# Attention on one core: another written-out order of the instructions, with other places for the early transfers, and two start-up copies of k that swap engines

## The chip, the cores and the metric

The kernel runs on one core of a Trainium2 chip. The metric is the device time of one launch in microseconds; lower is better. The engines of the core that matter here are TensorE (PE; its weight loads are listed as PEld), VectorE (DVE), ScalarE (ACT), GpSimd (POOL) and SyncE (SP), which only issues transfers. Each engine works through its own queue in order and waits for the others by semaphores.

## The reference

Grouped-query attention with 8 batches, 8 query heads, 2 key/value heads, 1024 positions and a head dimension of 64, in float32. Four query heads share one head of k and v.

```python
scale = 1.0 / np.sqrt(head_dim)
for g in range(n_kv_heads):
    q_group = q[:, q_start:q_end, :, :].copy()
    ...
    scores = scale * np.matmul(q_group, k_group.transpose(0, 1, 3, 2))
    scores_max = np.max(scores, axis=-1, keepdims=True)
    attn = np.exp(scores - scores_max)
    attn = attn / (np.sum(attn, axis=-1, keepdims=True) + 1e-08)
    output[:, q_start:q_end, :, :] = np.matmul(attn, v_group)
```

## The kernel before

A *job* is one query head of one batch; there are 64. The scores of a job are computed turned (keys in the partitions, queries along the free axis) in 8 chunks of 128 keys. A chunk is one *tile* of 128 x 1024 scores in one of three PSUM slots (`sp0` to `sp2`), written by two matmuls (L400). So there are 512 tiles, and each has to be raised to e. Two engines share that:

- 366 tiles go to ACT, one exponential each (L411, letter `x` in the order below), into one of 34 buffers `pt`.
- 146 tiles go to DVE, which builds e^x out of bits. The step `p` (L422) writes a scaled score as a 16-bit integer into the ring `ye` of 22 tiles. One or two neighbouring tiles form a *chain*. For a chain, `z` (L431) takes the fraction bits into the ring `zz`; a multiply of `zz` by `ye` follows, part of its columns on POOL (`G`, L448) and the rest on DVE (`m`, L457); `t` (L463) masks `ye` in place, which leaves the exponent part. The two rings together stand for e^x, and PE takes both as terms of one sum; for the last three jobs `+` (L474) adds them first.

PE then multiplies the tiles of a job with v (L491, letter `V`, three small products of 65 columns at a time; column 65 is a row of ones, which gives the sum of the weights). 7 output pieces of 128 queries share a PSUM bank; when they are done DVE takes the reciprocal of the sums (`r`, L560) and scales the pieces (`n`, L571), and SP stores a finished job (`S`). The first job is summed chunk by chunk as its tiles come (`E`, L529), the last one likewise (`L`). `F` is a small matmul on a zero tile, which keeps PE busy early on.

Transfers: POOL's queue issues casts of q, k and v to bf16 in DRAM (`X`/`q`, `Y`/`k`, `Z`/`v`; the capital ones first wait for the latest score matmul). SP's queue issues the turning loads of q (`T`) and k (`K`), the copy of k to the other half of the partitions (`C`) and the fill of v (`U`). A cast `qd8`, from job 6 on, brings two jobs at once; `kd` and `vd` are k and v of a batch and group.

What sets the order is a text, `ORDER`: one letter per step, walked once from left to right. `A` is the score of the next tile for ACT, `a` to `g` the score of a tile for DVE of the current job or up to six jobs ahead; the number is the PSUM slot. `G2,78` means that POOL multiplies 8 x 78 columns of the chain before the one before the last. `LENGTHS` gives the number of tiles in each chain. Every step goes into its engine's queue at the place where the walk meets it. A `G` besides waits for the DVE step that came before the latest `z`, `m`, `t` or `+`:

```python
tc.add_manual_dep(gps.ins, gate.ins.name, Sync, reason="the port goes to the step behind it")
```

Before the walk comes a written-out start (L280 to L313): k and q of job 0 are loaded straight, turned by PE against an identity, and copied out of PSUM into `k0` and `q0` by ACT and DVE.

Of the kernel before, what the change touches and what calls it, by code (L numbers as in the profile page):

```python
# [25 lines left out]
VVVVVG0,108nxd2A0TpVSVVxVVVVA1zd2xA0TG1,148pVVVVVxVVVVA1rnd2xA0pVSVVVVxVG0,36VVVA1zk2e2xA0pVVVG1,47V
VxVVVVVA1zq16d2xA0t3VVVVVG2,115rVxVpVA1VVVVxVVVnA0d2m2xVSVG1,71VpA1TVVxVVVVA0t2e2xG1,78pA1VVVVVxUVVA
0rze2TxVVG2,107VKpA1VVxVVVVVnA0A2xzq18VSVVVVVt3Ve1xA0G2,84pTVVVVCVxVVVA2rzd1xA0G3,172pVVVVVxVVVVVA2n
e1xA0pVVVVVVxVVVA2v2rt3A1xVVVm2VVVVVVVxe0A2G1,192pVVVxVVVVTA1ne0xA2pVSVVVVxVVVVA1rt2e0q20xA2pVVVG1,4
7VVxVVVVA1m1G0,106e0nxA2pVSVVVVxUVVVA1ze0xA2G1,78pVVVVVxVVVA1rze0xA2G2,72pVVVVxVVVTA1t3e0xVG1,192VpA  # L30
2VVVxVVA1ne0xVVpVSA2VVCVxVVVrA1m1q22A0t2xVVVVVt1VTVVVxVVG0,32nd2A1zVSVxVVG1,71A0pVVVxVVKVVA1zd2xA0G2
,78rpVVVVVxVVVVA1zd2xA0G3,75pTVVVVVxVVVA1nG2,18A2xVzVk3VSVVVVVt4Vxd0A1G3,191rpTVVVVxVVVVA2ne0xA1pVSV
VVVVxVVVA2m2q24A0xVVVVVVVrVt2xVVVVA1G3,30nd2xA0m3G1,71pSTVVVVVxVVVA1t3d2xA0G1,79pVVVVVxVVA1rzA2xVVVm
2VVVVVG1,106nd0xUA1pVVVVVxVVCVVA2m1q26A0xVVKVt2VVTVVVVxVt1d1A2G0,72pVVxVVVA0VVzxVv3VVVA1Tzd2xA0G2,18
4rpVVVVVxVVVVA1nd2xA0pSVVVVVxVVVVrA1t2d2xA0G1,71pVVVVVxVVVVzA1q28A2xVzVVVVVG3,114nd0xA1pVSVVVxVVVVA2
rTm3A0xG2,30VnVVVVVt3Se1xA2G2,71pVVVVVxVVVA0m2e1xA2G1,78pTVVVVVxVUVVA0rt2d1xA2G1,178pVVVVxVVVVA0nTd1
xA2pSVVVVVxVVVA0q30zA1CxVzVVVVVVVrG2,106nxd2A0pVVSVVxVVVVA1t3d2xA0KG2,71pVVVVVxVVVA1ze2xA0G3,79pVVVV
VxVVVA1rTzA2k4xVVt4VVVVVVG3,115xne0A1pVSVVxVVA2VVrVxm3Vq32VVVA0m2A1xVVVVVVVTVVG1,106nxe2A0pVSVVVxVVV
VVA1Tt3d2xA0G1,78pVVVVVVxVVVA1rt2A2xVVVm1VVVVG0,107nd0xA1pVVVVVxVVVVA2t1d0xVG0,78VpTA1VVVxVUVVA2rzA0
xVVq34zVVVVVVnxe1G2,71A2pVSVVVxVVKVVA0CG1,10rne1G1,98xA2pVVSVVVxVVVVA0t2v4e1xA2pTVVG1,47VVVxVVVA0ze1  # L40
xA2G2,78pVVVVVxVVVA0rm2G1,106e1nxA2pTVSVVVxVVVVA0t2e1xA2G1,71pVVVVVxVVVA0m1q36A1zxVVVVVG1,122VrVnVxd
2A0pSVVVVxVVVVA1t2e2xA0G1,71pVVVVVxVVVVA1ze2xA0G2,63pVVVVVVxVUVVVTzA1e2xG2,78rA0pVVVVVVxVVVA1t3A2xVz
VVVVTVVVG3,114ne0xA1pVSVVVxVVVKVA2rm3A0q38xzVVVVVVt4e1CxA2G3,225pVVVVVxVVVTA0nd1xA2rpSVVVVVxVVVVA0ne
1xA2m3G2,71SpVVVVVxVVVVA0t3k5A1xVVm2VVVVe2xG1,78A0rpVVVVVxVVVVA1zq40A2xVVzVVVVVVG3,106ne0xA1pVTVVVVx
VVVVA2t4e0xA1G3,72pVVVVVxVVVVVA2rG2,105ne0xA1pSVVVVVVxVUVVVm2A2e0xA1G1,78pVVVVVVxVVVA2rTt3d0xVVVG1,7
# [50 lines left out]
def kernel(  # L96
# [213 lines left out]
    nc.vector.tensor_copy(out=q0[:, 0, h:HS], in_=s0[:, 1, h:HS])  # L310
    nc.vector.tensor_copy(out=k0[:, 0, 0:128], in_=s2[:, 0, 0:128])
    nc.scalar.activation(out=k0[:, 0, 128:HS], in_=ops[1][:, 128:HS], func=AF.Copy)
    nc.vector.tensor_copy(out=k0[:, 1, :], in_=ops[0])  # L313
# [293 lines left out]
```

## Time and profile before

| | |
|---|---|
| runs | 352.6, 352.64, 353.29 us; median 352.64 |
| profiled execution | 352.72 us; its span, first to last instruction, 350.9 us |
| granted clock of TensorE, mean | 0.995 |
| first exponential on ACT starts | 6.27 us after the span's start |
| POOL's issues of casts | 52 in the queue; 128 GB/s mean over all transfers |

The span is what the profile covers; 1.8 us of the profiled time lie around it. In the profile's lines a row of the timeline has the start in the span, the duration, the engine, the line of the kernel, the operation, the tiles written and read, and a count of equal neighbours. A row of the groups has the busy time of all its instructions, the mean length of one in ns, and the idle time of the engine just before them. Instructions of one engine overlap by some 0.08 us, so a mean length is a little more than the step costs in a full queue.

### The profile page before, as it was taken

What the parts mean: (1) busy time and instruction counts of PE and PEld (TensorE: products, weight loads), DVE (VectorE), ACT (ScalarE), POOL (GpSimd) and SP (SyncE); (2) the same over time, 40 slices, a digit from 0 to 9 for tenths busy, and PEclk for the clock granted to TensorE, in tenths of its full rate; (3) what the DMA queues carried; (4) which work ended last, traced back from release to release, by engine and by line L of the source; (5) the groups of instructions that cost most, each with busy time, mean ns of one, the idle gap of its engine ahead of it and who ended that gap; (6) DMA issues with size and microseconds to landing.
All of it is one profiled execution on the core that took longest, in us unless ns stands there. A gap on an engine that the chain in (4) does not pass through costs nothing.

```text
span 350.9 us, 14187 instructions
## 1 busy us (share of the span) xinstructions
PE 340.2 (97%) x6268; PEld 225.7 (64%) x6268; DVE 342.1 (97%) x518; ACT 339.8 (97%) x370; POOL 288.6 (82%) x236
## 2 busy tenths in 40 slices
...
GB/s 150 123 151 178 108 152 138 137 135 95 149 147 116 154 151 131 118 131 138 147 122 112 151 156 133 119 136 158 122 136 138 116 148 98 113 83 86 48 84 102
DMA packets 96606, 44.84 MB, mean 128 GB/s; under 512 B 61184, under 2 KB 95360, under 8 KB 95744
## 3 DMA queue, kind: packets, MB, share of 16 engines
...
q8 instruction: 49, 0.80, 1.0%
...
q14 instruction: 13, 0.11, 0.2%
...
## 4 chain that ended last, share of the span: by engine, by line
PE 55%; DVE 30%; ACT 8%; issue 3%; DMA 2%; SPq 0%; DVEq 0%
PE ops L491 30%; PE sp L400 24%; DVE ye L422 15%; ACT pt L411 8%; DVE ye L463 4%; DVE zz L431 4%; DVE ost L571 3%; DVE zz L457 3%; DMA kt<-kd 2%; DVE rec L560 1%; PE ops L269 1%; PE sp L529 1%; PE sp L292 0%; DVE kt L313 0%; PE ops L304 0%
## 5 line engine op out<-in xcount | busy, mean ns | idle before, releaser
L411 ACT ACTIVATE pt<-sp 128x1024 bf16<-128x1024 f32 x366 | 337.3, 1052 | 3.4 <-PE sp L400 3.2
L448 POOL TENSOR_TENSOR zz<-ye,zz 128x568 bf16<-128x568 bf16 (+29 forms) x126 | 248.5, 1973 | 25.4 <-DVE zz L431 9.0
L422 DVE TENSOR_SCALAR ye<-sp 128x1024 uint16<-128x1024 f32 x146 | 177.1, 1213 | 1.3 <-PE sp L400 0.8
L400 PE MATMUL sp<-qt,kt 64*128 64x512 bf16 x1024 | 166.5, 383 | 4.3 <-ACT pt L411 3.0
L491 PE MATMUL ops<-va,pt 128*128 128x65 bf16 x2832 | 160.6, 194 | 0.0
L491 PEld LDWEIGHTS <-pt 128*128 128x128 bf16 x2832 | 120.5, 98 | 30.7 <-issue 30.7
L491 PE MATMUL ops<-va,zz 128*128 128x65 bf16 x1136 | 123.8, 194 | 0.0
L491 PE MATMUL ops<-va,ye 128*128 128x65 bf16 x1104 | 119.6, 194 | 1.3 <-DVE ye L463 1.3
L491 PEld LDWEIGHTS <-ye 128*128 128x128 bf16 x1104 | 83.9, 98 | 16.9 <-issue 14.8
L491 PEld LDWEIGHTS <-zz 128*128 128x128 bf16 x1136 | 86.5, 98 | 9.8 <-issue 9.5
L400 PEld LDWEIGHTS <-kt 64*128 64x128 bf16 x1024 | 51.6, 93 | 58.9 <-issue 34.9
L463 DVE TENSOR_SCALAR ye<-ye 128x2048 uint16<-128x2048 uint16 (+1 forms) x77 | 51.6, 676 | 0.0
L431 DVE TENSOR_SCALAR zz<-ye 128x2048 uint16<-128x2048 uint16 (+1 forms) x77 | 49.7, 657 | 0.1
L571 DVE TENSOR_TENSOR ost<-ops,rec 128x448 f32<-128x448 f32 (+2 forms) x73 | 44.4, 608 | 0.3
L457 DVE TENSOR_TENSOR zz<-ye,zz 128x2048 bf16<-128x2048 bf16 (+31 forms) x54 | 33.4, 622 | 0.0
L174 POOL DMA_DIRECT2D qd<-in_q_dram x34 | 23.7, 697 | 5.6 <-PE sp L400 4.6
L560 DVE RECIPROCAL rec<-ops 128x7 f32<-128x7 f32 (+2 forms) x73 | 14.1, 194 | 0.0
L443 POOL MEMSET tick<- 128x1 bf16 x52 | 9.7, 187 | 0.0
L174 POOL DMA_DIRECT2D vd<-in_v_dram x8 | 5.9, 735 | 0.0
L174 POOL DMA_DIRECT2D kd<-in_k_dram x8 | 5.7, 712 | 0.0
L269 PE MATMUL ops<-warm 128*128 128x512 bf16 (+1 forms) x12 | 3.5, 448 | 1.2 <-DVE warm L168 1.2
L529 PEld LDWEIGHTS <-pt 128*128 128x128 bf16 x96 | 3.4, 98 | 1.2 <-issue 1.2
...
## 6 DMA issues: line engine op xcount, KB each, us to landing
...
qt<-qd SPq DMA_TRANSPOSE x63, 4.2
...
```

The costliest lines, as they stand in the source:

```text
L174: return nc.gpsimd.dma_start(out=t.rearrange("(a x) d -> a (x d)", a=128), in_=src.rearrange("(a x) d -> a (x d)", a=128),)
L400: now = nc.tensor.matmul(sps[x][:, hf, :], lhsT=t[lo : lo + D, c // NH, ci % NH * 128 : (ci % NH + 1) * 128], rhs=qt[j][lo : lo + D, 0, :] ...
L411: exps.append(nc.scalar.activation(out=p, in_=where_s[(j, c)], func=AF.Exp, scale=scale))
L422: vec = nc.vector.tensor_scalar(out=ye[:, i, :, :], in0=where_s[(j, c)], scalar1=EXP_A, scalar2=EXP_B, op0=ALU.mult, op1=ALU.add,)
L431: vec = nc.vector.tensor_scalar(out=ch.tiles(zz), in0=ch.tiles(ye), scalar1=0x7F, scalar2=0x3F00, op0=ALU.bitwise_and, op1=ALU.bitwise_or,)
L443: tock = nc.gpsimd.memset(tick, 0.0) if any(old) else None
L448: gps = nc.gpsimd.tensor_tensor(out=z, in0=flat(ch.tiles(ye))[:, ch.cols : ch.cols + w], in1=z, op=ALU.mult)
L457: vec = nc.vector.tensor_tensor(out=z, in0=flat(ch.tiles(ye))[:, 0 : ch.cols], in1=z, op=ALU.mult)
L463: vec = nc.vector.tensor_scalar(out=ch.tiles(ye), in0=ch.tiles(ye), scalar1=0x7F80, scalar2=None, op0=ALU.bitwise_and,)
L491: ended[job] = nc.tensor.matmul(ops[g % 2][:, lo : lo + D + 1], lhsT=p[:, par, qs * 128 : (qs + 1) * 128], rhs=va[(b * G + h // HPG) % NVA ...
L560: vec = nc.vector.reciprocal(out=to, in_=sums)
L571: vec = nc.vector.tensor_tensor(out=to, in0=src, in1=by, op=ALU.mult)
```

## The change

`ORDER` and `LENGTHS` are replaced as a whole; the work is the same. There are still 366 exponentials and 146 tiles of DVE. There are 76 chains for 77 (70 of two tiles and 6 of one, for 69 and 8), 120 multiplies on POOL for 126 with 100256 columns for 99344, 58 multiplies on DVE for 54, and 6 of the small matmuls `F` for 3. The beginning of the text, before and after:

```diff
 ORDER = """
-A0IX3TY1a1xA2pxA0za1xKA2pX4E0E2TxFA0m0E3xA1za2t1E5FxpFA0E1xm0A1E6X5zxb2t1A0pE7E4xTA1rzxb2nG0,78A0pxX
-6A1Y2m1xb2A0G0,50pxA1Tt1Z1xA2zb0VVVt1VxVVG0,78VpA1VVxVVVVrA2zc0TG1,101xnVVCpA1SVVxVVVVX8VKA2rm1A0xG0
-,31nVVb1t1v1UxA2pVG0,46VVVVxVVVVA0m0Tq10c1zxA2VpVG0,56VVVVxVVVVA0t1Tc1xzA2G1,200pVVVVVVxVVVVA0rnc1xA
+A0IX3TY1a1xA2pxA0za1xA2TpX4E0E2xFA0m0E3xb1KzA2pE5FxFFA0E6m0xFA1b2zE7X5xpFA0xA1t2Tb2zE1pxG0,56A0xt2b1
+X6A2m1E4xG0,72pA0xA2rnb1Y2t1xA0zVTVVVpVxVG0,170VA2VVVxVVrCnb0A1pTVVxSVA2VVVVm0xVX8VVVt1A0b1t0Z1xA2rV
+zVVVv1VVxVVpVA0TVG0,145VxVVVA2nb1VxUVpA0VVVVxVVKA2m0q10A1VzxVVVVVVVt1Vc0xG0,191A2rpVVVVVxVVVTA1nc0xA
...
@@
-    nc.vector.tensor_copy(out=k0[:, 0, 0:128], in_=s2[:, 0, 0:128])
-    nc.scalar.activation(out=k0[:, 0, 128:HS], in_=ops[1][:, 128:HS], func=AF.Copy)
+    nc.scalar.activation(out=k0[:, 0, 0:128], in_=s2[:, 0, 0:128], func=AF.Copy)
+    nc.vector.tensor_copy(out=k0[:, 0, 128:HS], in_=ops[1][:, 128:HS])
     nc.vector.tensor_copy(out=k0[:, 1, :], in_=ops[0])
```

The first place is the start. DVE's queue before, from the copy of the second half of q0 to the first `p`:

```order
L310 CAST qt<-sp_141 128x256
L311 CAST kt<-sp_143 128x128
L313 CAST kt<-ops_126 128x512
L422 TENSOR_SCALAR ye<-sp_177 128x1024
L431 TENSOR_SCALAR zz<-ye 128x1024
```

DVE's queue there after the change:

```order
L310 CAST qt<-sp_141 128x256
L312 CAST kt<-ops_127 128x384
L313 CAST kt<-ops_126 128x512
L422 TENSOR_SCALAR ye<-sp_177 128x1024
L431 TENSOR_SCALAR zz<-ye 128x1024
```

The copy of 384 columns stands where that of 128 stood; ACT has the one of 128 where it had the one of 384.

The second place is POOL's queue from the first multiply of chain 4 on, some 19 to 25 us into the span before (`L174` rows are casts that it issues). Before:

```order
L448 TENSOR_TENSOR zz<-ye,zz 128x624
L448 TENSOR_TENSOR zz<-ye,zz 128x808
L174 DMA qd_491<-in_q_dram 16x8192
L448 TENSOR_TENSOR zz<-ye,zz 128x248
L174 DMA vd_0_522<-in_v_dram 16x8192
L448 TENSOR_TENSOR zz<-ye,zz 128x368
L174 DMA qd_566<-in_q_dram 16x8192
```

After, from the multiply of chain 4 to that of chain 5:

```order
L448 TENSOR_TENSOR zz<-ye,zz 128x1360
L174 DMA qd_487<-in_q_dram 16x8192
L174 DMA vd_1_507<-in_v_dram 16x4096
L174 DMA vd_0_529<-in_v_dram 16x8192
L448 TENSOR_TENSOR zz<-ye,zz 128x1160
```

Chain 4 has one multiply for two, three casts follow on it in a row (the cast of v for group 1 stood earlier before), and chain 5 has one multiply of 1160 columns where it had two, of 248 and 368, with a cast between them.

The third place is DVE's queue around chain 4's `t` (the `L463` of 2048 columns). Before, from the `p` of tile 7:

```order
L422 TENSOR_SCALAR ye<-sp_449 128x1024
L560 RECIPROCAL rec<-ops_393 128x7
L457 TENSOR_TENSOR zz<-ye,zz 128x616
L571 TENSOR_TENSOR ost<-ops_393,rec 128x448
L463 TENSOR_SCALAR ye<-ye 128x2048
L422 TENSOR_SCALAR ye<-sp_518 128x1024
```

After, from the same tile's `p`:

```order
L422 TENSOR_SCALAR ye<-sp_445 128x1024
L457 TENSOR_TENSOR zz<-ye,zz 128x688
L463 TENSOR_SCALAR ye<-ye 128x1024
L463 TENSOR_SCALAR ye<-ye 128x2048
L560 RECIPROCAL rec<-ops_392 128x7
L431 TENSOR_SCALAR zz<-ye 128x2048
L422 TENSOR_SCALAR ye<-sp_503 128x1024
```

Chain 3's `t` now stands directly ahead of chain 4's, and chain 5, which has two tiles for one, is begun (`L431`) behind it and not ahead of it.

More of the change, by code (lines that the diff above doesn't have):

```diff
@@ L26 @@
[L26 to L45, printed above, removed]
@@ new lines @@
+2pSVVVVxVVVVm0q12A1c0zxA2pVG0,64VVVxVVVVA1rt1c0xVA2G0,192pVVVxVVVTA1nc0xA2pSVVVVVxVVVA1rzc0xA2pVG0,5
+6VVVCVxVVA1t1d0xVG0,184pA2TVVVxA1nc0xpA2STVVVVVxVUVVVVm0q14zA1c0xrA2pG0,63VVVVVVxVVVA1t1c0xVG0,106Vp
+A2VVVxVA1nA0xzVk2VSVVVVVVzVc2xA1G2,78rKpVVVVVxVVVVVA0m2G1,105nc2xA1pVSVVVVVxVVVVA0t2Tq16d2xA1zVVVVG2
+,78pVVxVVVVTA0VVxVrVm2VA1G1,106nc2xVVpA0SVVVxVVVA1m1A2TxVVVt2VVVVVVVt1xc0A1G0,78pVVVVxVVVVVA2rzc0xA1
+TG1,178VpVVVVCVxVVVVA2nc0xA1pVSVVVVVxVVVVA2q18rt1d0xA1KpG0,93VVVVVxVVUVVA2nA0xVzv2VVVVVVzxe1A2G2,80T
@@ new lines @@
+pVVVVxVVVA0rm2d1xA2G1,73pVVVVVxVVVA0t2e1xA2G1,183pVVVVVxVVVA0Tnd1xVVpVSA2VVxVVA0rq20t1A1VxVVzVVVVVVG
+1,106nxd2A0pVSVVVxVVVVVA1ze2xA0G2,71pTVVVVVxVVVVA1m2A2rxt2VVVVVVG1,111Vnd0xUA1pSVVVVVxVVVVTA2ze0xA1G
+2,78pVVVVVxVVVVA2rzq22e0xA1pVVG3,47VVCVxVVKVVA2m3G2,114nd0xA1pSVVVVVxVVVA2rt3e0xVVG2,106pA1TVVVxVVVV
+A2ne0xVm2VG1,71SVpA1VVxVVVA2t2k3e0xA1pVG1,54VVVVxVVVrA2m1e0xA1G0,106pTVVVVxVVVA2nA0xVzVq24VSVVVVt2d1
+xA2G1,71pVVVVxVVVVVA0ze1xA2G2,71pVVVVVVxVVVVA0m2re1t2xA2G1,191pVTVVVVVxUVVVA0nd1xA2pSVVVVVxVVVVA0rze
@@ new lines @@
+1xA2G2,65pTVVVVCVxVVVA0q26zA1xVt3VVVVVG2,114nd2xA0pVVVVxVVVKVA1rzA2v3xA0zVVVVVVxVm4VVVVVVVG3,106ne1x
+A2pVTSVVVVVxVVVVA0t4d1xA2G3,71pVVVVVVxVVVA0m3e1G2,247rxVpVVTA2VxVVA0nd1VxpVVSA2VVVxVVrVnA0A1xVm2Sq28
+t3VVVVVVt2xd2A0TG1,71pVVxVVVVA1zd2xA0G2,78pVVVVVxVVVVVA1rm2d2xA0G1,71pVVVVVVxVUVVA1t2e2xVG1,106VpVA0
+VVxVVVVTnA1A2CxzVq30VSVVVVVzVd0xA1G3,79pVVVVVxVVKVVVA2rne0G2,100xA1pVSVVVVVxVVVA2t3e0xG2,78A1pTVVVVV
+xVVVA2rm2k4A0xzVVVVVVt3Vxd1A2G2,197pVVVVxVVVVA0ne1xA2pSVVTVVVxVVA0rm1A1q32xVVVVVTVVVG2,30nVxVVVm2A2S
@@ new lines @@
+t1d0xVVG0,78VpA1VVxVVVA2rt2e0xA1G0,71pVVVVVxVVVVA2Tzd0xA1G1,107pVVVVVxVUVVVA2nA0xzVVVVVVVVt2Vxe1KA2G
+1,191rpVVVVxVVVVA0ne1CxA2pSVVVVxVVVVTA0m1q34A1zxVVVVVv4t2VVxe2A0rpG1,177VVVVxVVVA1ne2xA0pSVVVVVxVVVA
+1ze2xA0G2,79pVVVVxVVVA1rzA2xVVG2,30VnVVVVVt3q36xSe0A1pVVG2,47VxVVVVVA2Tze0xA1G3,78pVVVVVVxVVVVA2rm3A
+0xVG2,30VnVVTVVVVt3e1xSUA2G2,71pVVVVVxVVVVA0zd1xA2G3,71pVVVVVxVVVA0zd1xA2G4,71pVVVVVxVVVA0m4q38rA1t4
+xVVVKTzVVCVVxe2G4,114nA0VpVVSVxVVVA1VrxVm4VVVA2TG3,106ne0xA1pVSVVVVxVVVA2t4e0xA1G3,79pVVVVVxVVVA2rm3
@@ new lines @@
+k5A0xzVVVVVVt4Vd1xA2G3,227pTVVVVVxVVVVA0ne1xA2rpSVVVVVxVVVA0nA1xVm1q40VVVVVVxe2A0m3G2,78pVVVVxVVVVA1
+rt3e2xA0G2,178VpVVVVxVVUVVA1nd2xA0pVSVVVVVxVVVVA1t1e2xA0G0,71pTVVVVVVxVVVVt2A1e2xG0,84A0rpTVVVVVxVVV
+VA1zq42A2xVVm1VVVCVVG0,115nd0xA1pVSVVVVxVVKVVA2rzA0v5xVVVzVVVVVVxVt3VVVA1G2,106nd2xA0pTSVVVVVxVVVVzA
+1d2xm3A0G2,71pTVVVVVxVVVVA1t3e2xA0G2,121pVVVVVxVVVA1rnA2xVVVVzVSq44VVVVxe0m3A1G2,190rpVVVVVxVVVTVA2n
+d0xA1pSVVVVVVxVVVVA2t3e0xA1G2,66pVVVVVVxVVVzA2e0xG2,114rA1pVVVVVxVUVVTA2nA0xVt3VVSVVVVVq46m2VxVVVVVz
@@ new lines @@
+A1d2xG2,191rA0pVVVVVVxVVA1nCe2VxVpVSVA0VVxVVVm2A1e2t3xVVVVG1,78KpA0VVxVVVVA1rt2e2xA0G1,178pVVVVVxVVV
+VA1nTe2xA0pVVVVVxVVVA1k6zTA2xVVzVVq48VVVVt3Vxe0A1G2,191rpVVVxVVVVVA2nd0xA1pVSVVVVxVVVVA2Tzd0xA1G3,65
+pVVVVVxVVVA2rt3A0xVVVzVVVVVG3,106e1nxA2pVVVSVVxVVVVA0ze1xA2G4,78pVVVVVVxVVUVVA0rm4A1q50xVzVKVVVVVVt5
+xe2A0G4,191pVVVVCVxVVVA1ne2xA0pSVTTVVVVxVVVVA1rm4v6A2xzVVVVVVVt5e0xA1G4,191pVVVVVxVVVVA2nd0xA1rpSVVV
+VVVxVVVm4A2A0G3,30nxA1t4q52VVSVVVxVm2VVVVVVVxc2A0G3,192rpVTVVVVxVVVVA1ne2xA0pSVVVVVVxVVVA1m3e2t2xVVV
@@ new lines @@
+VG1,71pA0VVxVUVVVA1t3e2xA0G1,78pTVVVVxVVVVVrA1zd2xA0G2,107pVVVVVVxVVVA1TnA2xVzVq54VSVVVVt3e0xA1KG2,7
+8pVCVVVVxVVVVA2rzd0xA1G3,178pVVVVVxVVVVTA2nd0xA1pVVVVVxVVVVrA2t3d0xA1G2,106pVVVVVxVVVTA2nA0xVm1Vk7SV
+VVVe1xA2G2,78pVVVVxVVVVA0rm2q56A1xt1VVVVVVt2e2xA0G0,71pVVVxVVVVA1ze2xA0G1,185pVVVVVxVVVVA1nTe2xrA0pS
+VVVVVxVUVVA1ze2xVG1,106VpA0VVVxVVA1nA2Vxm1VVSVVVVVVq58t2Ve0xA1pVVG0,59VVVxVVVVVA2rt1d0xA1G0,106pVVVV
+VVxVVVVA2TnCA0xVzVv7VSVVVVze1xA2KG2,78pVVVVVxVVVVA0rm2e1G1,106nxA2VpVVSVVVxVVVVTA0t2d1xA2G1,78pVVVVV
@@ new lines @@
+VxVVVVTA0rm1A1q60xVzVVVVVVG1,109Vnd2xA0pSVVVVVxVVVVA1t2e2xA0G1,78pVVVVVxVVVVA1Trm1A2xVzVVVVVG1,109Vn
+d0xA1pSVVVVVxVVVVA2t2e0xA1G1,78pVVVVVxVVVA2rze0xVVG2,69VpA1VVxUVVVA2nG1,24A0xzVq62VVVTVVt3Vxe1A2G2,1
+91rpVVVxVVVVA0nCe1xKA2pVSVVVVxVVVA0m2q63A1zxVVVVt3VVe2xG2,118A0rpTVVVVVxVVVA1nA2xVm1VVSVVVVd0xA1G2,7
+1pVVVVVxVVVVA2t1e0xA1G2,67pVVVVVxVVVVVA2rt2d0xA1G0,106pVVVVVVxVVVA2nA0xVzVVSVTVVVVzVxVVVVzA1e2xG3,11
+4VrVpA0VVVxVVVA1ne2xm3A0G2,71SpVVVVVxUVVVVA1t3Td2xG2,81A0pVVVVVxVVA1rzA2xVVVm3VVVVG2,106nd0CxA1pVSVV
```

32 lines of the change are left out of this document (6 added, 26 removed).

## The prediction

> **What bounds the kernel now.** I read the page's busy shares first, then the busy time by stretches, then the timeline of each engine in the one stretch that stands out. The page's first section, and then the stretches (us from the span's start; length, busy time and instructions of PE, PEld, DVE, ACT, POOL; granted clock; DMA share; GB/s):
>
> ```profile
> span 350.9 us, 14187 instructions
> PE 340.2 (97%) x6268; PEld 225.7 (64%) x6268; DVE 342.1 (97%) x518; ACT 339.8 (97%) x370; POOL 288.6 (82%) x236
> ```
>
> ```profile
> 20.00:25.00 5.00, 4.08 (x65) 2.33 (x61) 5.00 (x9) 5.00 (x7) 4.88 (x6) 1.00 0.87 152
> 25.00:30.00 5.00, 4.29 (x61) 2.91 (x63) 4.54 (x7) 2.57 (x3) 2.49 (x4) 0.66 1.11 183
> 30.00:35.00 5.00, 4.89 (x95) 3.12 (x92) 4.58 (x6) 4.87 (x6) 4.06 (x2) 1.00 1.01 157
> 60.00:340.00 280.00, 278.91 (x5300) 188.18 (x5300) 279.45 (x414) 279.82 (x305) 244.54 (x194) 1.00 0.67 125
> ```
>
> From 60 to 340 us three engines are full at once: DVE lacks 0.55 us of 280, ACT 0.18, PE 1.09. Nothing can be won there except by taking work away. Between 25 and 35 us it is different: ACT lacks 2.43 + 0.13 us and PE runs at 0.66 of its clock. The timelines of ACT, DVE and POOL there (start, duration, what; in brackets the idle time before it and what ended it), and the line of the waits between 12 and 35 us for PE:
>
> ```profile
> 27.22 1.94 ACT L411 ACTIVATE pt<-sp 128x1024 bf16<-128x1024 f32 x2 [1.59 <-PE sp L400]
> 30.13 11.16 ACT L411 ACTIVATE pt<-sp 128x1024 bf16<-128x1024 f32 x12 [0.97 <-PE sp L400]
> ```
>
> ```profile
> 23.33 2.33 DVE L463 TENSOR_SCALAR ye<-ye 128x2048 uint16<-128x2048 uint16 x1
> ...
> 30.35 1.22 DVE L422 TENSOR_SCALAR ye<-sp 128x1024 uint16<-128x1024 f32 x1 [0.81 <-PE sp L400]
> ```
>
> ```profile
> 20.66 1.86 POOL L448 TENSOR_TENSOR zz<-ye,zz 128x808 bf16<-128x808 bf16 x1
> 22.46 0.55 POOL L174 DMA_DIRECT2D qd<-in_q_dram  x1
> 23.03 0.66 POOL L448 TENSOR_TENSOR zz<-ye,zz 128x248 bf16<-128x248 bf16 x1
> 23.64 0.55 POOL L174 DMA_DIRECT2D vd<-in_v_dram  x1
> 24.20 0.89 POOL L448 TENSOR_TENSOR zz<-ye,zz 128x368 bf16<-128x368 bf16 x1
> 25.03 0.72 POOL L174 DMA_DIRECT2D qd<-in_q_dram  x1
> ```
>
> ```profile
> PE ops L491 <- DVE ye L463: 1.3, 1, 1.3
> ```
>
> A `t` step of 2048 columns (L463, the masking of ye) lasts 2.33 us. It begins inside POOL's multiply of 248 columns and ends 0.57 us after the multiply of 368 columns has ended (24.20 + 0.89 = 25.09; 23.33 + 2.33 = 25.66), as if it had run only from there. Its own wait, on chain 4's multiplies, was over at 22.52, when the one of 808 columns ended (20.66 + 1.86). So DVE was held by a train of POOL instructions (multiply, cast issue, multiply). PE then waits 1.3 us for this `t`, its clock drops, ACT waits 1.59 and 0.97 us for scores, and DVE itself waits 0.81 us.
>
> **The change, part by part.** Durations, by shape (busy us of the group, mean ns of one, idle before):
>
> ```profile
> L463 DVE TENSOR_SCALAR ye<-ye 128x2048 uint16<-128x2048 uint16 x69 | 48.2, 704 | 0.0
> L431 DVE TENSOR_SCALAR zz<-ye 128x2048 uint16<-128x2048 uint16 x69 | 46.3, 684 | 0.0
> L457 DVE TENSOR_TENSOR zz<-ye,zz 128x2048 bf16<-128x2048 bf16 x9 | 10.8, 1214 | 0.0
> L448 POOL TENSOR_TENSOR zz<-ye,zz 128x624 bf16<-128x624 bf16 x17 | 29.2, 1719 | 3.3 <-DVE zz L431 1.6 <-DVE ye L422 0.8
> L448 POOL TENSOR_TENSOR zz<-ye,zz 128x848 bf16<-128x848 bf16 x10 | 20.6, 2058 | 1.7 <-DVE zz L431 1.4
> L463 DVE TENSOR_SCALAR ye<-ye 128x1024 uint16<-128x1024 uint16 x8 | 3.4, 438 | 0.0
> L457 DVE TENSOR_TENSOR zz<-ye,zz 128x1024 bf16<-128x1024 bf16 x5 | 3.4, 683 | 0.0
> L431 DVE TENSOR_SCALAR zz<-ye 128x1024 uint16<-128x1024 uint16 x8 | 3.4, 421 | 0.0
> ```
>
> *The place of the long `t`.* In the new order chain 4 gets one multiply of 1360 columns on POOL. Chain 5 is begun only after chain 4's `t`, so none of its multiplies can stand ahead of that `t`. POOL's queue there holds the issues of qd8, vd1 and vd0 behind the 1360, and the next multiply (1160 columns) waits for a step of DVE that itself comes after the `t`. The train multiply, cast, multiply is gone from this place. Such a `t` lasts 0.70 us by the mean, so 2.33 - 0.70 = 1.63 us return, and with them DVE's 0.81 us of waiting: 2.44 us. ACT's side gives 1.59 + 0.97 = 2.56, which agrees. PE's idle time of the three stretches is 0.92 + 0.71 + 0.11 = 1.74 us, and its lower clock from 25 to 30 us holds up to 5 x 0.34 = 1.7 more, so PE can follow. Since all three engines are full later, time won here should reach the end.
>
> By the Trainium skill (SBUF — State Buffer, "Who interferes with whom"), GpSimd and a VectorE step in a two-port mode share one pair of ports; the one that issues first holds it for its whole instruction, and the other is blocked. By that, the `t` would have begun when the multiply of 248 ended; the trace shows it held over two more POOL instructions, so it agrees on the block and not on its length. By the rule a block in the new burst would cost one issue at most, 0.55 us, and the sum below would then be 350.1 + 0.55 = 350.6 and not the 352.5 of the first rival.
>
> *DVE's amount of work.* Chains go from 77 to 76: 70 of two tiles and 6 of one, where 69 and 8 were. That is one pair of 2048-column steps more (48.2/69 + 46.3/69 = 1.37 us) and two pairs of 1024 less (2 x (3.4 + 3.4)/8 = 1.70): -0.33 us. POOL takes 912 columns more from DVE's multiplies (100256 for 99344), at (1214 - 683)/1024 = 0.52 ns each: -0.47. But DVE has 58 multiplies for 54, each with a fixed part of 683 - 531 = 152 ns: +0.61. Sum -0.19 us, all on a full engine. If the fixed part is hidden by overlap it is -0.80; this is the lower bound, and 0 the upper.
>
> *POOL.* 120 multiplies for 126 and 912 columns more: at (2058 - 1719)/224 = 1.51 ns a column and 1719 - 944 = 775 ns fixed, -6 x 0.775 + 1.38 = -3.3 us, on an engine that is idle 18% of the span. Worth 0 by itself. Nothing of before prices where its ends fall against DVE's steps; that is the main unknown, taken up below.
>
> *PE and ACT.* The same 512 score pairs, 366 exponentials and 5200 small products behind them; PE gets three warming matmuls more, in stretches of the first 20 us where it waits anyway: 0.
>
> *The two copies of k.* The rows of the start, PE, DVE, ACT:
>
> ```profile
> 5.23 0.64 PE L304 MATMUL ops<-ident,k 128*64 128x128 bf16 x8
> 5.80 0.86 PE L400 MATMUL sp<-qt,kt 64*128 64x512 bf16 x6
> ```
>
> ```profile
> 4.91 0.42 DVE L310 CAST qt<-sp 128x256 bf16<-128x256 f32 x1 [0.25 <-PE sp L292]
> 5.25 0.28 DVE L311 CAST kt<-sp 128x128 bf16<-128x128 f32 x1
> 5.91 0.69 DVE L313 CAST kt<-ops 128x512 bf16<-128x512 f32 x1 [0.38 <-PE ops L304]
> ```
>
> ```profile
> 5.34 0.49 ACT L312 ACTIVATE kt<-ops 128x384 bf16<-128x384 f32 x1 [0.26 <-PE ops L292]
> 6.27 1.94 ACT L411 ACTIVATE pt<-sp 128x1024 bf16<-128x1024 f32 x2 [0.45 <-PE sp L400]
> ```
>
> The first score begins at 5.80, 0.27 us after the first block of k is copied (5.53) but just as the eight turning matmuls ahead of it on PE are out (5.23 + 0.64 = 5.87). An earlier first block therefore wins nothing, at best those 0.27. The copy of 384 columns takes on DVE, between the rows of 256 (0.42) and 512 (0.69), about 0.55 us: 5.25 to 5.80, and the next copy waits for PE until 5.91 anyway. If that cover of 0.11 us were gone, DVE would start 0.1 us later. I take 0.
>
> *Early transfers.* The turn of kd0_1 goes behind that of qd3 on SP's queue, but job 4's first score, which needs it, stands 13 exponentials behind the turn, as before. The turn of q for job 2 leads its first score by 7 exponentials (8 before), at 1.94 - 0.97 = 0.97 us at most each some 6 us. No transfer becomes the last to arrive. 0.
>
> *The end.* After the last exponential DVE has one more normalization of 448 columns ahead of the last two; it was 0.5 us earlier in the queue with less behind it. The rows of before: PE's last products and DVE's last steps.
>
> ```profile
> 346.50 0.42 PE L529 MATMUL sp<-va,pt 128*128 128x65 bf16 x8
> 346.96 0.21 DVE L560 RECIPROCAL rec<-sp 128x8 f32<-128x8 f32 x1 [0.16 <-PE sp L529]
> 343.62 0.62 DVE L571 TENSOR_TENSOR ost<-ops,rec 128x448 f32<-128x448 f32 x1
> ```
>
> DVE waited 0.16 us there, and the moved step costs 0.62: between -0.16 and +0.46 us. The pair of scores of the last tile on DVE stands one exponential earlier, which pays for it: 0.
>
> **The sum.** The profiled execution took 352.72 us, 0.08 above the median of 352.64. 352.72 - 2.44 - 0.19 = 350.09. A `t` that begins inside one POOL multiply is also held a little:
>
> ```profile
> 17.84 0.58 DVE L463 TENSOR_SCALAR ye<-ye 128x1024 uint16<-128x1024 uint16 x1
> 18.12 1.00 POOL L174 DMA_DIRECT2D vd<-in_v_dram  x1
> ```
>
> 0.58 for a mean of 0.44. Two of these for the new early burst (the `t` steps of chains 3 and 4 beside three issues) add 0.3: **350.4 us**.
>
> **Rivals.** *The same stall again.* The burst qd8, vd1, vd0 stands right beside two `t` steps and a `z`. If one of them is held as the 2.33 us step was, the 2.44 us are lost again: 350.1 + 2.4 = 352.5, no change. For it: three issues in a row. Against it: at 18.12 an issue beside DVE's steps was the one that gave way (1.00 us for 0.55).
>
> *PE sets the pace.* If only PE's idle 1.74 us can be won, since its clock is back at 1.00 from 30 us on: 352.72 - 1.74 = 351.0, faster all the same.
>
> *Slower: a longer train.* Later in POOL's new queue (the cast of kd for batch 2) stand multiplies of 848, a cast, 624 and 840 columns. A `t` or `z` that begins at the head of such a train and is held to its third member loses 2.06 + 0.72 + 1.72 = 4.5 us, less what POOL has done: 350.1 + 4.5 = 354.6 at most. It decides from 3.2 us of holding on, since 350.1 + 3.2 is 0.2% above the median. For it: every multiply's end has moved against DVE's steps, all through the kernel. Against it: in the 280 us from 60 on DVE lost next to nothing, though POOL's queue was as dense (244.54 of 280 us).
>
> **Chances.** 0.2% (0.7 us) is about what a measurement of this kernel can tell from no change. The forecast (349.4 to 351.2) gets 0.48, PE's pace (351.0 to 351.9) 0.13; both are faster: 0.61. The same stall again 0.17, all of it within 0.2%. The longer train 0.22, slower. The range leaves out the last half of the longer train and a little below: its low end is the sum with -0.80 for -0.19, 349.5, and the 0.16 of the end; its high end the train at 3.5 us. The likeliest case alone spans 349.4 to 351.2.
>
> **What would show it.** Right: no L463 or L431 row above 0.9 us before 40 us; ACT's gaps of 1.59 and 0.97 us gone and the granted clock 1.00 from 25 to 30 us; DVE's busy time lower by about 1.8 us (1.63 + 0.19); the first exponential at 6.2 to 6.4 us, the way from the last exponential's end to the end of the span unchanged. Wrong: a fast DVE step of 2 us or more anywhere, or PE waiting for POOL's multiplies (L448), which it hardly does now.

## The result, and the profile after

The changed kernel takes 349.68 us, the median of 6 runs (348.91 to 350.82), against 352.62 us for the kernel before (352.3 to 353.29): a ratio of 0.9923, 95% interval 0.9901 to 0.9944. It is faster by 2.9 us, 0.8%. Ratios here and below leave out the few runs that took over 1.5% longer than the fastest of their kernel. Its profiled execution took 349.65 us, with a span of 347.8 us and a mean granted clock of 0.999. The first lines of its page, and its busy time by stretches (columns as in the prediction: length, PE, PEld, DVE, ACT, POOL, granted clock, DMA share, GB/s):

```profile
span 347.8 us, 14190 instructions
PE 339.3 (98%) x6271; PEld 226.0 (65%) x6271; DVE 339.9 (98%) x520; ACT 339.1 (97%) x370; POOL 288.0 (83%) x228
```

```profile
20.00:25.00 5.00, 5.00 (x98) 3.33 (x95) 4.96 (x10) 5.00 (x7) 4.25 (x5) 1.00 0.84 116
25.00:30.00 5.00, 5.00 (x90) 3.22 (x91) 5.00 (x9) 5.00 (x6) 4.28 (x3) 1.00 0.97 210
30.00:35.00 5.00, 4.91 (x84) 2.99 (x84) 5.00 (x8) 5.00 (x7) 4.33 (x4) 1.00 1.01 116
60.00:340.00 280.00, 279.69 (x5300) 188.96 (x5297) 279.81 (x419) 280.00 (x305) 243.89 (x189) 1.00 0.72 125
```

The hole between 25 and 35 us is closed: ACT is busy for 5.00 of 5.00 us where it had 2.57, and the clock is 1.00 where it was 0.66. The timeline of DVE around chain 4's `t`, and that of POOL beside it:

```profile
22.29 1.01 DVE L463 TENSOR_SCALAR ye<-ye 128x1024 uint16<-128x1024 uint16 x2
23.22 0.19 DVE L560 RECIPROCAL rec<-ops 128x7 f32<-128x7 f32 x1
23.34 0.64 DVE L431 TENSOR_SCALAR zz<-ye 128x2048 uint16<-128x2048 uint16 x1
```

```profile
21.92 0.55 POOL L174 DMA_DIRECT2D qd<-in_q_dram  x1
23.21 1.35 POOL L174 DMA_DIRECT2D vd<-in_v_dram  x2 [0.74 <-PE sp L400]
24.57 2.41 POOL L448 TENSOR_TENSOR zz<-ye,zz 128x1160 bf16<-128x1160 bf16 x1
```

Two `t` steps, of 1024 and of 2048 columns, take 1.01 us together, where the one of 2048 alone took 2.33. ACT's timeline over the whole span, after; then the two rows of before that begin with its two gaps behind the early hole; then the group of exponentials in each profile (busy, mean ns | idle before), before first:

```profile
6.18 336.79 ACT L411 ACTIVATE pt<-sp 128x1024 bf16<-128x1024 f32 x366 [0.89 <-PE sp L400]
```

```profile
58.88 243.91 ACT L411 ACTIVATE pt<-sp 128x1024 bf16<-128x1024 f32 x265 [0.16 <-ACT pt L411]
302.96 43.48 ACT L411 ACTIVATE pt<-sp 128x1024 bf16<-128x1024 f32 x47 [0.18 <-PE sp L400]
```

```profile
L411 ACT ACTIVATE pt<-sp 128x1024 bf16<-128x1024 f32 x366 | 337.3, 1052 | 3.4 <-PE sp L400 3.2
```

```profile
L411 ACT ACTIVATE pt<-sp 128x1024 bf16<-128x1024 f32 x366 | 336.8, 1044 | 0.9 <-PE sp L400 0.9
```

After the change ACT runs its 366 exponentials in one unbroken row; it is now the pace of the kernel from 6.18 to 342.97 us. That gives the account of the span, profile against profile:

| where | us |
|---|---|
| the two early gaps of ACT, 1.59 + 0.97 | -2.56 |
| its two small gaps later, 0.16 + 0.18 | -0.34 |
| the exponentials themselves, 337.3 to 336.8 | -0.5 |
| first exponential, 6.27 to 6.18 | -0.09 |
| last exponential's end to the end of the span, 350.9 - 346.44 = 4.46, now 347.8 - 342.97 = 4.83 | +0.37 |
| sum | -3.1 |

### The profile page after: what moved, and what is told of

Read it like the earlier page. It is cut to its first block, busy times and chain, and to the rows that moved or that the text cites. A ratio compares the mean times of both kernels' runs of the same rounds, so it can differ in the third digit from the quotient of the medians.

```text
span 347.8 us, 14190 instructions
## 1 busy us (share of the span) xinstructions
PE 339.3 (98%) x6271; PEld 226.0 (65%) x6271; DVE 339.9 (98%) x520; ACT 339.1 (97%) x370; POOL 288.0 (83%) x228
## 4 chain that ended last, share of the span: by engine, by line
PE 65%; DVE 11%; issue 1%; DVEq 0%
PE ops L491 36%; PE sp L400 28%; DVE ye L422 6%; DVE ye L463 2%; DVE ost L571 1%; DVE zz L431 1%; DVE zz L457 1%; PE sp L529 1%; DVE rec L560 0%; DVEq L602 0%; DVEq L463 0%
## 5 line engine op out<-in xcount | busy, mean ns | idle before, releaser
L411 ACT ACTIVATE pt<-sp 128x1024 bf16<-128x1024 f32 x366 | 336.8, 1044 | 0.9 <-PE sp L400 0.9
L448 POOL TENSOR_TENSOR zz<-ye,zz 128x848 bf16<-128x848 bf16 (+26 forms) x120 | 248.6, 2072 | 21.1 <-DVE zz L431 7.8
L491 PE MATMUL ops<-va,zz 128*128 128x65 bf16 x1136 | 126.0, 194 | 0.0
L491 PE MATMUL ops<-va,ye 128*128 128x65 bf16 x1104 | 121.8, 194 | 0.0
L463 DVE TENSOR_SCALAR ye<-ye 128x2048 uint16<-128x2048 uint16 (+1 forms) x76 | 50.0, 664 | 0.0
L431 DVE TENSOR_SCALAR zz<-ye 128x2048 uint16<-128x2048 uint16 (+1 forms) x76 | 49.4, 660 | 0.0
L457 DVE TENSOR_TENSOR zz<-ye,zz 128x2048 bf16<-128x2048 bf16 (+29 forms) x58 | 33.6, 583 | 0.0
L174 POOL DMA_DIRECT2D qd<-in_q_dram x34 | 22.2, 653 | 6.3 <-PE sp L400 5.5
L443 POOL MEMSET tick<- 128x1 bf16 x50 | 11.6, 232 | 0.0
L174 POOL DMA_DIRECT2D vd<-in_v_dram x8 | 5.7, 713 | 0.7 <-PE sp L400 0.7
L174 POOL DMA_DIRECT2D kd<-in_k_dram x8 | 5.4, 676 | 0.3 <-PE sp L400 0.3
L269 PE MATMUL ops<-warm 128*128 128x128 bf16 (+1 forms) x15 | 4.0, 402 | 1.2 <-DVE warm L168 1.2
```

The costliest lines, as they stand in the source:

```text
L174: return nc.gpsimd.dma_start(out=t.rearrange("(a x) d -> a (x d)", a=128), in_=src.rearrange("(a x) d -> a (x d)", a=128),)
L411: exps.append(nc.scalar.activation(out=p, in_=where_s[(j, c)], func=AF.Exp, scale=scale))
L431: vec = nc.vector.tensor_scalar(out=ch.tiles(zz), in0=ch.tiles(ye), scalar1=0x7F, scalar2=0x3F00, op0=ALU.bitwise_and, op1=ALU.bitwise_or,)
L443: tock = nc.gpsimd.memset(tick, 0.0) if any(old) else None
L448: gps = nc.gpsimd.tensor_tensor(out=z, in0=flat(ch.tiles(ye))[:, ch.cols : ch.cols + w], in1=z, op=ALU.mult)
L457: vec = nc.vector.tensor_tensor(out=z, in0=flat(ch.tiles(ye))[:, 0 : ch.cols], in1=z, op=ALU.mult)
```

## The experiments

Theory: the early loss of before comes from the `t` that is held by the train multiply, cast, multiply on POOL. Rivals: the place of the early transfers makes it, or the copies of k, or something spread over the whole order. The edits below are to `ORDER`. As a measure of the early stretch I use the time from the first exponential's start to that of the 41st, from ACT's rows in each profile: 39.43 us before and 36.94 after.

### The train on POOL

**One multiply for the two of chain 5, in the order of before:**

```diff
-rm1A0xG0,31nVVb1t1v1UxA2pVG0,46VVVVx
+rm1A0xnVVb1t1v1UxA2pVG0,77VVVVx
```

> The order of before, with one edit: chain 5's two multiplies on POOL (248 and 368 columns, with a cast of v between them) become one of 616 where the one of 368 stood. Theory (a train multiply, cast, multiply on POOL holds the fast DVE step): without the multiply of 248 ahead of it the t step of chain 4, which lasted 2.33 us, lasts 0.7, ACT's two waits of 1.59 and 0.97 us go, and the time falls by 2.4 us to about 350.2. Rival (the step is held by something else, such as the loads that land just then): it stays near 2.3 us and the time at 352.6.

350.86 us against 351.98 for before on this chip; ratio 0.9983 [0.9958, 1.0009]. DVE's and ACT's rows:

```profile
23.72 0.70 DVE L463 TENSOR_SCALAR ye<-ye 128x2048 uint16<-128x2048 uint16 x1
```

```profile
6.53 44.44 ACT L411 ACTIVATE pt<-sp 128x1024 bf16<-128x1024 f32 x48 [0.62 <-PE sp L400]
```

The `t` takes its 0.70 us, ACT has no early gap, and the early stretch is 36.95 us, that of the changed kernel. But the interval does not tell its times from those of before, whose own 35 runs here lie in two groups, 13 from 350.8 to 351.3 us and 16 from 352.4 to 353.7, with six between. So the loss of 2.5 us seems not to be in every execution. The edited kernel's own 12 runs spread too: nine lie from 350.2 to 352.0 us and three from 353.9 to 357.0. The profile is of one of the nine; what the three lost is not on record.

**The cast of v behind both multiplies:**

```diff
-b1t1v1UxA2pVG0,46VVVVx
+b1t1UxA2pVG0,46v1VVVVx
```

> The order of before, with one edit: the cast of v for batch 1 is issued behind the multiply of 368 columns, not between the multiplies of 248 and 368, which then follow each other directly. Theory (any POOL work in a row holds the step to the train's end): the t step ends about 0.55 us sooner (1.8 us for 2.33), and the time falls by about 0.5 us. Rival A (the cast in the train is what keeps the port): the step is let in after the first multiply, lasts 0.7 to 1.0 us, and the time falls by 2 us or more. Rival B (something outside POOL): no change.

352.02 us; ratio 1.0023 [0.9992, 1.0055]. Its profile is of an execution of 355.96 us. DVE, POOL, and the row of PE that was late:

```profile
23.81 0.85 DVE L463 TENSOR_SCALAR ye<-ye 128x2048 uint16<-128x2048 uint16 x1
```

```profile
23.43 1.97 POOL L448 TENSOR_TENSOR zz<-ye,zz 128x248 bf16<-128x248 bf16 x2
```

```profile
38.50 1.04 PE L400 MATMUL sp<-qt,kt 64*128 64x512 bf16 x4 [3.22 <-DMA qt<-qd]
```

The `t` began inside the first multiply, as in before, and was held by 0.15 us only. The two multiplies took 1.97 us together, where 0.66 and 0.89 stood before: this time POOL gave way to the `t`. For the step that is the expectation's rival A; the fall of 2 us that goes with it did not come. This execution lost 3.2 us at another place: PE waited for the turned q of job 8.

**A longer train, the second multiply in two:**

```diff
-A2pVG0,46VVVVx
+A2pVG0,23G0,23VVVVx
```

> The order of before, with one edit: the multiply of 368 columns on POOL is cut into two of 184 that follow each other. Theory (the t step is held to the end of the train): the train ends later by the fixed part of one more multiply, 0.3 to 0.5 us, so the t step lasts 2.6 to 2.8 us and the time rises by 0.3 to 0.5 us. Rival A (it is let in between two multiplies without a cast between them): it ends at the first multiply of 184, lasts about 1.9 us, and the time falls by about 0.4 us. Rival B (something outside POOL): no change.

351.47 us; ratio 0.9991 [0.997, 1.0012]. DVE's and POOL's rows, and PE's late one:

```profile
23.54 0.68 DVE L463 TENSOR_SCALAR ye<-ye 128x2048 uint16<-128x2048 uint16 x1
```

```profile
22.84 0.77 POOL L448 TENSOR_TENSOR zz<-ye,zz 128x248 bf16<-128x248 bf16 x1
23.55 0.77 POOL L174 DMA_DIRECT2D vd<-in_v_dram  x1
```

```profile
35.72 0.61 PE L400 MATMUL sp<-qt,kt 64*128 64x512 bf16 x4 [0.79 <-DMA qt<-qd]
```

Here the `t` began 0.07 us before the multiply's end, not 0.36 as in before, and was not held. So this execution does not test what a longer train costs a `t` that it holds, and neither the theory nor its rivals are decided. Again PE waited for q of job 8.

**The kernel before, once more:**

> The kernel before, unchanged, for another profile and a spread of its times on this chip. Theory: its early loss differs from execution to execution, so this profile shows the t of chain 4 at another length than 2.33 us or a wait of PE for qt of 0.5 us or more, and its times spread over 350.8 to 353.5 us. Rival (one fixed stall): the t lasts 2.2 to 2.4 us again, and the times lie within 0.3% of 352.6 us.

352.67 us (350.98 to 353.13), ratio 1.0012 [0.9992, 1.0032]; two of its 12 runs lie at 351.0, ten from 352.4 on. DVE's and POOL's rows:

```profile
23.48 2.34 DVE L463 TENSOR_SCALAR ye<-ye 128x2048 uint16<-128x2048 uint16 x1
```

```profile
23.19 0.66 POOL L448 TENSOR_TENSOR zz<-ye,zz 128x248 bf16<-128x248 bf16 x1
23.80 0.55 POOL L174 DMA_DIRECT2D vd<-in_v_dram  x1
24.37 0.89 POOL L448 TENSOR_TENSOR zz<-ye,zz 128x368 bf16<-128x368 bf16 x1
```

The expectation that this profile would show something else was wrong: the hold came again, to 0.01 us, the early stretch is 39.46 us, and the profiled execution (352.83 us) belongs to the upper group. The rival of one fixed stall fits the times of ten of the twelve runs, and not the two of 351.0.

All the traces together show what goes with a hold. In the kernel before and its variants, 12 `t` steps begin more than 0.2 us before the end of a multiply on POOL. Three begin 0.36 to 0.38 us before it; they are the ones that are held over the multiply, the cast and the next multiply. Nine begin 0.28 to 0.29 us before it; they are held by some 0.15 us, to the end of that multiply alone, and POOL's next instruction gives way. For one of the nine, in the kernel with the cast behind, the next instruction is a multiply; for the other eight, one in each of eight profiles, it is a cast. The `t` at 17.84 us that the prediction shows is of these eight: it begins inside this multiply of before, which ends at 18.13 us, and ahead of the cast at 18.12 us.

```profile
17.18 0.95 POOL L448 TENSOR_TENSOR zz<-ye,zz 128x400 bf16<-128x400 bf16 x1
```

So a cast behind the multiply is not enough to hold a `t` over it. In these 12 cases the moment at which the `t` begins separates the long holds from the short ones. No run moved that moment alone, so whether the make-up of the train matters as well stays open.

### The turning loads on SP's queue

**In the order of before, one multiply, and the store of job 0 and the fill of v behind the turn of q for job 8:**

```diff
-VVCpA1SVVxVVVVX8VKA2rm1A0xG0,31nVVb1t1v1UxA2pVG0,46
+VVCpA1VVxVVVVX8VKA2rm1A0xnVVb1t1v1xA2pVG0,77
...
-VVVVA0t1Tc1xzA2G1,200
+VVVVA0t1TSUc1xzA2G1,200
```

> The order of before, with two edits at the early transfers: chain 5's two multiplies on POOL become one of 616 columns, and on SP's queue the store of job 0 and the fill of v for group 1 go behind the turn of q for job 8, which then is issued about 2 us sooner. Theory (before loses its early time in two ways that change from run to run: a fast DVE step held by POOL, and PE waiting for the turn of job 8, which landed at 34 to 38 us where its first score is due at 35): both are gone, the median falls to 350.0 us, and the runs lie closer together. Rival (the late turn does not matter): as with the one multiply alone, a median of 350.9 us and a spread up to 353 and more.

350.25 us (349.61 to 351.51) against 352.65; ratio 0.9942 [0.9924, 0.996]. ACT has no early gap:

```profile
6.00 40.83 ACT L411 ACTIVATE pt<-sp 128x1024 bf16<-128x1024 f32 x44 [0.39 <-PE sp L400]
```

Two edits in an order that is otherwise the old one bring 2.4 of the 3.2 us that the changed kernel had on this chip (349.44, below). The theory's 350.0 is met within 0.3 us, and the runs lie close together. The early stretch is 36.98 us, where the one multiply alone had 36.95. That kernel ran on another chip, so what the queue's edit adds, fewer late runs by the theory, is read across two chips.

**The queue's edit alone, the train left in:**

```diff
-VVCpA1SVVxVVVVX8VKA2rm1
+VVCpA1VVxVVVVX8VKA2rm1
...
-b1t1v1UxA2pVG0,46
+b1t1v1xA2pVG0,46
...
-VVVVA0t1Tc1xzA2G1,200
+VVVVA0t1TSUc1xzA2G1,200
```

> The order of before with one edit on SP's queue alone: the store of job 0 and the fill of v for group 1 stand behind the turning load of q for job 8, POOL's train multiply 248, cast, multiply 368 is left as it is. Theory (two separate early losses, the queue of turns and the held t): the turn of job 8 lands at 31 to 33 us for 34 to 38, PE waits for no qt, the chain 4 t is held in some executions and not in others; 350.4 to 351.4 us, between before and the kernel that has both edits (350.25). Rival (the train alone makes the loss): no change, 352 to 352.7 us, with the t at 2.3 us. Second rival (the queue alone makes it): as with both edits, 350.1 to 350.4 us.

352.54 us against 352.42; ratio 0.9997 [0.9975, 1.002]. The `t`:

```profile
23.52 2.34 DVE L463 TENSOR_SCALAR ye<-ye 128x2048 uint16<-128x2048 uint16 x1
```

No gain: the rival that the train alone makes the loss fits, and my 350.4 to 351.4 was wrong. The turn of job 8 lands at 31.97 us for 34.62, and nobody has use for it, since the held `t` delays everything behind it. Where the `t` is held, the turns have time enough; where it is not, they can be what comes late next: PE waited for the turn of job 8 by 3.2, 0.8 and 0.2 us in the profiles with the cast behind, the longer train and the one multiply.

**In the changed order, the turn of q for job 7 behind the fill of v and the turn of k:**

```diff
-A0TVG0,145VxVVVA2nb1VxUVpA0VVVVxVVKA2m0q10
+A0VG0,145VxVVVA2nb1VxUVpA0VVVVxVVKTA2m0q10
```

> The changed kernel, with one edit: on SP's queue the turn of q for job 7 goes behind the fill of v for group 1 and the turn of k for batch 1, where it stood before the change. Theory (the place of the early turns decides the early stage): it is issued at about 31 us, not 23, lands at about 36 us, and job 7's first score, due at about 33 us, waits; PE waits 2 to 3 us for qt and the time rises to 352 to 353 us. Rival (the turns have room, the gain came from POOL's queue alone): no change from 349.7 us.

355.23 us; ratio 1.0079 [1.0049, 1.0108] against before, and 5.8 us above the changed kernel on the same chip. The profile (353.25 us) has PE's wait and ACT's gap:

```profile
36.32 0.42 PE L400 MATMUL sp<-qt,kt 64*128 64x512 bf16 x2 [2.53 <-DMA qt<-qd]
```

```profile
37.59 1.02 ACT L411 ACTIVATE pt<-sp 128x1024 bf16<-128x1024 f32 x1 [2.74 <-PE sp L400]
```

The direction is as expected, the size larger. So in the new order the place of one early turn is worth more than the whole change. The old order did not depend on that turn: job 7's first score stands behind 41 exponentials there, and behind 30 in the new order. Issue and landing of the two turns in the trace, in us, with the early stretch:

| kernel | q of job 7 | q of job 8 | early stretch |
|---|---|---|---|
| before (`t` held) | 26.63, 34.01 | 29.40, 34.62 | 39.43 |
| queue's edit alone (`t` held) | 25.24, 31.26 | 27.38, 31.97 | 39.48 |
| longer train (`t` free) | 27.67, 35.26 | 29.75, 35.58 | 37.93 |
| one multiply and queue | 25.09, 31.40 | 26.79, 31.72 | 36.98 |
| changed kernel | 23.03, 29.68 | 31.32, 36.24 | 36.94 |
| changed kernel, second profile | 23.33, 32.28 | 35.50, 39.16 | 37.06 |
| its turn of job 7 late | 30.80, 36.27 | 32.72, 37.49 | 40.67 |

In the changed order job 8's turn lands later than in before, and is hardly waited for: its first score comes five exponentials later there (36 exponentials ahead of it, for 31). In the second profile of the changed kernel, where it lands at 39.16 us, PE waits 0.2 us for it.

### The other parts

**The copies of k alone, in the kernel before** (the three lines of the start as in the diff of the change):

> The order of before; only the two copies of k in the start are swapped between ScalarE and VectorE. Prediction's step: 0, at best 0.27 us less. From the trace of after, where the first exponential starts 0.09 us sooner: 0 to 0.1 us less. Rival (the swap carries a large share of the 3 us): a fall of 0.5 us or more.

352.45 us against 351.98; ratio 1.0009 [0.9988, 1.003]. In its profile (350.87 us) the `t` was free, 0.68 us. The early stretch is 38.05 us all the same; the windows show where it lost time:

```profile
15.00:20.00 5.00, 3.64 (x35) 1.95 (x34) 5.00 (x7) 4.74 (x6) 4.96 (x6) 0.82 0.85 157
20.00:25.00 5.00, 4.71 (x67) 2.84 (x65) 3.96 (x10) 4.18 (x5) 4.15 (x5) 0.83 1.02 203
```

The granted clock is 0.82 and 0.83 from 15 to 25 us, and ACT lacks 0.26 + 0.82 = 1.1 us there; PE's scores ended its gaps. This looks like a third way to lose early time in that order. What lowered the clock is not known, and no run tested it.

**The changed kernel with the old copies of k, and the changed kernel again:**

> The changed order with the two copies of k as they were before. Theory (the order carries all of it, the copies 0.1 us): 349.8 us. Rival (the copies carry 0.5 us or more): 350.2 us or more.

> The changed kernel once more, beside the others. Both theories: about 349.7 us, some 2.3 us under the median of before. In its trace PE waits for no turning load of q, and no fast DVE step lasts 0.9 us or more before 40 us.

349.47 us (349.3 to 349.7) and 349.44 us (349.0 to 351.11) against 352.65: ratios 0.992 [0.9898, 0.9942] and 0.9926 [0.9899, 0.9954]. The copies carry nothing that these times resolve. In the second profile of the changed kernel no fast step of DVE lasts more than 0.77 us before 40 us, as expected, but PE waits for a turning load, if only by 0.2 us, which it was not to do.

**The changed kernel with the end in another order** (the last normalization before the last two jobs, and the store behind it, ahead of the last `t`):

```diff
-VVt1VVxVVt0VA2+1A1xVVrVL2,0+0L3,0L4,0xnL5,0L0,0rL1,0nSL6,
+VVt1VVxrnSVVt0VA2+1A1xVVVL2,0+0L3,0L4,0xL5,0L0,0rL1,0nL6,
```

> The changed kernel, with the last normalization before the last two jobs and the store behind it moved ahead of DVE's last long t. Theory (the way behind the last exponential is longer by 0.37 us since that normalization and its store stand late): 4.83 us of that way go back to about 4.5, the time is 349.2 to 349.4 us. Rival (the way is set by the last products, and the late store costs nothing): 4.8 us as before, 349.5 to 349.7 us.

349.35 us (348.63 to 349.66); ratio 0.9926 [0.9902, 0.9949]. The issue on SP's queue of the first of the two last stores, in the changed kernel and here:

```profile
344.21 0.46 SPq L573 DMA_DIRECT2D out_dram<-ost  x1
```

```profile
344.47 0.34 SPq L573 DMA_DIRECT2D out_dram<-ost  x1
```

From that issue to the end of the span it is 347.8 - 344.21 = 3.59 us in the changed kernel, 347.7 - 344.47 = 3.23 here, and 350.9 - 347.65 = 3.25 in before. In the trace the late store's 0.3 us come back. But the stretch differs between executions of the unchanged end as well: it is 347.6 - 344.06 = 3.54 us in the second profile of the changed kernel and 347.8 - 344.49 = 3.31 in the one with the old copies of k, which has the late store too. So one profile of the new end does not settle it, and neither does the time, 0.1 below that of the changed kernel on another chip.

**With that end, and on SP's queue the turn of k ahead of the fill of v and the store of job 0 behind the turn for job 8:**

```diff
-A1pTVVxSVA2VVVVm0xVX8
+A1pTVVxVA2VVVVm0xVX8
...
-b1VxUVpA0VVVVxVVKA2m0q10
+b1VxKVpA0VVVVxVVUA2m0q10
...
-VVVTA1nc0xA
+VVVTSA1nc0xA
```

> The changed kernel, with the same end, and on SP's queue the turn of k ahead of the fill of v and the store of job 0 behind the turn of q for job 8. Theory (in the changed order the turn of job 8 still leads its first score by only some 3 us, and this does not hold PE in most executions): the turn lands 0.5 to 1.5 us earlier, nothing waits for it either way, and the time is that of the kernel with the new end alone, 349.2 to 349.4 us. Rival (late transfers still cost something in the changed order): 348.6 to 349.1 us.

349.34 us, but 348.58 to 353.42; ratio 0.9943 [0.9913, 0.9973]. The median lies where the theory had it. In its profile (350.5 us) the turn did not land sooner, and PE did wait for a transfer:

```profile
36.33 0.40 PE L491 MATMUL ops<-va,pt 128*128 128x65 bf16 x8 [1.24 <-DMA va<-vd]
```

The turn for job 8 landed at 37.64 us, later than 36.24, and PE waited for the fill of v that I had put behind the turn of k. The order of these transfers in the changed kernel leaves little room.

## Why the prediction was right, and where its steps were not

- **The forecast** of 350.4 us is 0.7 us above the 349.68 measured, which lies inside its likeliest case of 349.4 to 351.2; the direction and the main place are right. The low end of the range, by the terms that the prediction gives for it, is 349.5 - 0.16 = 349.3. There is luck in the size: the profile that the prediction read, and all six runs of before beside the result, lie in the upper of two groups of times that this kernel has. Against the lower group (350.8 to 351.3 us on another chip) 349.68 us would be a gain of 1.1 to 1.6 us, and the step on the long `t` would have had nothing to win if that group is the free `t`, as is inferred below.
- **The place of the long `t`, -2.44 us (-2.56 on ACT's side): right.** The early stretch fell by 2.49 us, ACT's two gaps by 2.56. The term is the same with the `t` alone freed: 36.95 us with one multiply. What the step did not see is that this stall is one of several outcomes. Of the kernel before, 16 of 35, 10 of 14 and 16 of 29 runs on the three chips lie between 352.2 and 354.1 us, one at 356.96, the others below. The three profiles that show the hold took 352.72 to 353.34 us; the ones of that order with a free `t` took 349.9 to 350.9, but for 355.96 where q came late. That the groups of unprofiled runs are the held and the free `t` is inferred from this. The reason that the prediction gives, a train of multiply, cast and multiply, is half of it: the hold spans that train in all three profiles, but the same train did not hold a `t` that began later in the first multiply.
- **Early transfers, 0: the step that failed in its reasoning.** It looked at jobs 2 and 4 and found that no transfer becomes the last to arrive. Once the stall is gone the turn for job 8 is the next to be late, by 0.8 and 3.2 us in two profiles of variants of the old order, and in the new order the turn for job 7, by 2.5 us when it was moved. The term came out near 0 because the new order issues job 7's turn 3.6 us sooner, now that this job's first score comes 11 exponentials earlier, and asks for job 8's five later. The prediction did not work this out, so that 0 is luck.
- **DVE's amount of work, -0.19 (bounds -0.80 to 0): the size was off, within its bounds.** DVE's busy time fell by 342.1 - 339.9 = 2.2 us, of which 2.33 - 0.68 = 1.65 is the long `t`; 0.55 is left. Four profiles of variants of the old order with a free `t` have 340.3 to 340.5 us, 0.4 to 0.9 above the 339.6 to 339.9 of three in the new order. No run shows that this reached the end: ACT sets the pace now.
- **The allowance of 0.3 for short holds: not paid.** The `t` steps beside the casts took 1.01 us for two; POOL waited 0.74 us for a score while the longer of them ran, so the three issues did not meet them as one burst. The one longer early step, 0.77 us for a mean of 0.68, is a `z` elsewhere:

```profile
31.84 0.77 DVE L431 TENSOR_SCALAR zz<-ye 128x2048 uint16<-128x2048 uint16 x1
```

- **Nothing to win from 60 to 340 us: off by some 0.7.** Every profile of the old order took 299.5 to 299.9 us from the 41st exponential's start to the last one's, every one of the new 298.7 to 298.8. Two gaps of ACT, at 58.88 us, just ahead of the window, and at 302.96 us, make 0.34 of it; they stand at the same two exponentials in every profile of the old order and in none of the new. The rest is exponentials that ran shorter in sum. Which step of the new order does it was not tried.
- **The end, 0: off by +0.37 in this profile**, inside its bounds (-0.16 to +0.46) but by another road: DVE's moved step did not delay the last products, which ended 0.5 us after the last exponential in both profiles. The first of the last two stores is issued 1.2 us after that exponential in both, so the longer way lies behind this issue. That the late store behind the moved step delays them is likely, not shown: with the same late store that stretch took 3.31 to 3.59 us in four profiles, for 3.25 in before.
- **The copies, 0: right** as far as the two pairs of kernels resolve it. The first exponential came at 6.18 us, a hair below 6.2 to 6.4; with the same start it came at 5.88 to 6.40 in other executions.
- **The rivals.** The same stall did not return. PE's pace did not bind: ACT shows no wait for a score behind its first exponential, though PE was busy for 5.00 of 5.00 us from 20 to 30 us. No longer train held a step: the longest `t` or `z` in the profile is 0.88 us.
- **The rule of the Trainium skill** (SBUF — State Buffer, "Who interferes with whom") says that the engine which issues first has the shared pair for one whole instruction. The kernel with the cast behind agrees: the `t` began inside one multiply, was held to about its end, and the next gave way. So do the eight `t` steps that were held to a multiply's end ahead of a cast. Before, before again and the queue's edit do not: three times the `t` came out 0.56 or 0.57 us after the end of the third POOL instruction (25.82 for 25.26 in before again). The measurement decides for this train. What separates the two kinds of case in these traces is the moment at which the `t` begins, 0.36 to 0.38 or 0.28 to 0.29 us before the multiply's end; why this moment should matter was not settled.
